# A hybrid encoder: another order of stages, and the recurrence's transposes made by VectorE in 32x32 blocks and moved by DMAs

## The chip, the cores and the metric

The kernel runs on one core of a Trainium2 chip. Its time is the device time of one execution, in microseconds; the median of several executions is given. Profiles show one execution.

## What is computed

The input is 512 tokens of 1024 float32 values. Layer 0 normalises (RMS), projects into a gated MLP branch and a windowed attention branch, and projects the gated branches back. Layer 1 is a gated linear recurrence over 16 heads of 128 channels, in both directions; then a norm per head, a gate, an output projection and a final RMS norm. Cut to layer 1's core:

```
f = lb + (1 - lb) * sigmoid(f_logit);  k = 1 - f;  g = log f
bcum = cumsum of g in a chunk;  q_t = q * exp(bcum);  k_t = k * exp(-bcum)
a = tril(q_t @ k_t.T);  o = a @ v  +  q_t @ state;  state = decay * state + k_end.T @ v
o = o_forward + o_backward;  o = o * rsqrt(mean(o * o) + eps) * gain
x = x + (o * silu(z)) @ w_out;  out = rms_norm(x, final gain)
```

## The kernel before

**Products.** Every large product is float32 split into a high and a low part: high x high, high x low, low x high, three matmuls of 128x512 for each block of 128 rows (`mm3`, L215). Weights come in pieces of 512 KB: a DMA on SP's queue (`_dma`, L53 and L55), a cast to the high part by ScalarE (L66) and the low part by VectorE (L67). Four raw buffers and four split buffers are there; loads are issued seven pieces ahead of use, splits three ahead (`ahead`).

**Two kinds of product.** `t_block` makes one block of 128 channels by 512 tokens from one piece, 24 matmuls. `nat_blocks` makes 512 tokens by 512 channels from four pieces, 96 matmuls. `out_blocks` projects the outputs of some heads back and adds them to the four token tiles `xs` (n heads: 8 blocks of 3n matmuls).

**Layer 1.** Four groups J of four heads. A group first makes the values `iv` and the gates `zv` (two `nat_blocks`, 192 matmuls), then, from the second group on, projects the outputs of earlier heads (`out_blocks`: heads 0 to 3, 4 to 7, and in the last group 8 and 9), then for each head three `t_block`s (query and the two forget gates) and starts the head's recurrence `hgrn`. Behind the last head stand the projections of heads 10 to 13 and of 14 and 15. These last two heads' projection also makes the final norm (`finish`, `store`, L792 to L808).

**The side work.** `hgrn`, layer 0's attention and its mixer are generators: they issue some instructions, then `yield n`, which means "go on after n ticks". A tick comes with every eighth matmul of `mm3` (`SLOT`), and at most three generators run (`tick`, `spawn`, L190 to L205). `tick_until` makes ticks without matmuls until a result is there. So the text fixes where in TensorE's stream each piece of a head stands:

```
prepare q, k (ScalarE, VectorE, POOL)  yield 7   L655-L683
a = masked products; 6 key transposes  yield 1   L692-L710
k.T @ v                                yield 1   L720
state u; a @ v                         yield 1   L731-L735
q @ state                              yield 1   L739-L741
head norm, gate                        yield 4   L746-L751
4 output transposes; split ahi, alo    yield 1   L755-L758
```

The six key transposes (L708, L709) go to PSUM and are copied by ScalarE to `kn` (L710); the four output transposes (L755) go to PSUM, from where ScalarE and VectorE make `ahi` and `alo` (L757, L758). POOL multiplies `qf` into `qb` and `qf` (L680, L682) for heads 0 to 13.

**Order.** The framework plans each engine's order from costs that it estimates: an instruction whose operands are not there yet can be passed by a later one of the same engine. Inside `manual_schedule` the named engines keep the order of the text. On the chip each engine runs its list in that order.

**Layer 0.** `evac_va` (L420) normalises the gated branch's values right behind their products, on VectorE and POOL.

Of the kernel before, what the change touches and what calls it, by code (L numbers as in the profile page):

```python
# [18 lines left out]
P = 128  # L19
S = 512  # L20
# [9 lines left out]
WARM = 10  # L30

# [61 lines left out]
def tile_encoder(ctx, tc, x, xT, nge, wie, lng, lnb, ws, bs, sink, woe, ngo, wio, gaf, gab, hng, woo, fng, out):  # L93
# [89 lines left out]


# [5 lines left out]
    def tick():  # L190
        while waiting and len(side) < 3:
            side.append([waiting.popleft(), 1])
        for job in list(side):
            job[1] -= 1
            if job[1] <= 0:
                try:
                    job[1] = next(job[0])
                except StopIteration:
                    side.remove(job)

    def spawn(gen, delay=1):
        if len(side) < 3:
            side.append([gen, delay])
        else:
            waiting.append(gen)  # L205
# [77 lines left out]
    def act_pair():  # L283
        return [act.tile([P, S], F32R, tag=n, name=n, bufs=6) for n in ("ahi", "alo")]
# [39 lines left out]
    with ExitStack() as c0:  # L324
# [94 lines left out]

        def evac_va(nh):  # L420
            def f(t, ps):
                nc.scalar.copy(va[t][:, ts(nh, 512)], ps)
                nc.vector.bn_stats(out=st[t][:, nh], in_=ps)
                if nh == 1:
                    mv = small.tile([P, 2], F32, tag="mv", name="mv")
                    nc.vector.bn_aggr(out=mv, in_=st[t])
                    v = small.tile([P, 1], F32, tag="lnv", name="lnv")
                    nc.vector.tensor_scalar(out=v, in0=mv[:, 1:2], scalar1=rq2[:, t:t + 1], scalar2=EPS,
                                            op0=ALU.mult, op1=ALU.add)
                    r = inv_sqrt(v, 1, "ln")  # L430
                    nc.gpsimd.tensor_tensor(out=r, in0=r, in1=rq[:, t:t + 1], op=ALU.mult)
                    nc.vector.tensor_scalar(out=va[t], in0=va[t], scalar1=mv[:, 0:1], scalar2=r,
                                            op0=ALU.subtract, op1=ALU.mult)
                    nc.vector.tensor_tensor(out=va[t], in0=va[t], in1=lngb, op=ALU.mult)
                    nc.gpsimd.tensor_tensor(out=va[t], in0=va[t], in1=lnbb, op=ALU.add)
            return f
# [21 lines left out]

        kThi = l0.tile([P, 2, S], F32R, tag="kThi", name="kThi")
# [3 lines left out]
        for j in range(2):  # L463
            ps = t_block()
# [187 lines left out]
    def hgrn(h, sq, sg, iv, zv):  # L652
        hl = h % 4
        hs = ts(hl, P)
# [48 lines left out]
        kn = l1.tile([P, 3, 2, P], F32, tag="kn1", name="kn1", bufs=1)  # L703
        for b in range(2):
            nj = 2 if b == 0 else 1
            ps = sm_bank()
            for j in range(nj):
                nc.tensor.transpose(ps[:, ts(2 * j, P)], ck(kf, 2 * b + j), ident)  # L708
                nc.tensor.transpose(ps[:, ts(2 * j + 1, P)], ck(kb, 3 - 2 * b - j), ident)  # L709
            nc.scalar.copy(kn[:, 2 * b:2 * b + nj].rearrange("p j d t -> p (j d t)"), ps[:, :nj * 256])  # L710
        yield 1
        pk = []
        for b in range(2):
            nj = 2 if b == 0 else 1
            ps = sm_bank()
            for j in range(nj):
                for d in range(2):
                    jj = 2 * b + j
                    n = jj if d == 0 else 3 - jj
                    nc.tensor.matmul(ps[:, ts(2 * j + d, P)], lhsT=kn[:, jj, d], rhs=iv[:, n, hs], start=True, stop=True)  # L720
            pk += [ps[:, j * 256:(j + 1) * 256].rearrange("p (d v) -> p d v", d=2) for j in range(nj)]
        yield 1
# [14 lines left out]
        yield 1  # L737
# [5 lines left out]
        yield 1  # L743
# [19 lines left out]
    for J in range(4):  # L763
        iv = l1.tile([P, NT, 512], F32, tag="iv", name="iv", bufs=2)
        zv = l1.tile([P, NT, 512], F32, tag="zv", name="zv", bufs=2)

        def evac_i(t, ps):
            nc.scalar.copy(iv[:, t], ps)

        def evac_z(t, ps):  # L770
            nc.scalar.activation(zv[:, t], ps, AF.Sigmoid)
            nc.vector.tensor_tensor(out=zv[:, t], in0=ps, in1=zv[:, t], op=ALU.mult)

        nat_blocks(evac_i)
        nat_blocks(evac_z)
        if J:
            n = 2 if J == 3 else 4
            tick_until(lambda: 4 * (J - 1) + n - 1 in acat1)
            out_blocks([acat1[4 * (J - 1) + k] for k in range(n)])
# [12 lines left out]
    def finish(t, nh):  # L792
        if nh == 0:
            sst[t] = small.tile([P, 2], F32, tag="ss", name="ss")
        junk = l1.tile([P, 512], F32, tag="o2", name="junk", bufs=1)
        square_half(t, nh, sst[t], junk)
        if nh == 1:
            if t:
                store(t - 1)
            scales.append(rstd_halves(sst[t], "nr"))  # L800

    scales = []

    def store(t):
        for cs in halves:
            xv = xs[t][:, cs]
            nc.vector.scalar_tensor_tensor(out=xv, in0=xv, scalar=scales[t], in1=gain2[:, cs], op0=ALU.mult, op1=ALU.mult)
            nc.sync.dma_start(out=out[ts(t, P), cs], in_=xv)  # L808

# [38 lines left out]
```

## Time and profile before

| | |
|---|---|
| median of 3 runs | 1029.49 us (1029.46 to 1029.79) |
| the profiled execution | 1029.34 us |
| its span, first to last instruction | 1027.6 us |
| mean granted TensorE clock | 0.997 of full speed |
| layer 1 with the end | from about 372 us on |

The page gives each engine's busy time and instructions; the timeline gives start, duration and operation of each instruction, and in brackets how long its engine stood idle before it and what ended that. Matmuls overlap, so the distance between two starts is read, not the duration of one.

### The profile page before, as it was taken

The page shows a single profiled execution, that of the slowest core. Times are in us where ns is not written, and L with a number is a line of the kernel's source. Part 1 is how long each engine was busy: PE and PEld are TensorE (multiplying, and loading weights), DVE is VectorE, ACT ScalarE, POOL GpSimd, SP SyncE. Part 2 cuts the span into 40 slices and gives each one's busy share as a digit, 9 for nine tenths or more (in the row PEclk, how much of TensorE's full clock was granted, in tenths as well). Part 3 has the DMA queues.
Part 4 walks back from the last instruction along what each step waited for, and adds up shares of the span by engine and source line. Part 5 has one row for each costly group of instructions (what it writes and reads, how often), then busy time and mean ns, then how long its engine had stood idle before and what let it go on. Part 6 is the DMA issues. An engine that isn't in the chain of part 4 may idle for free.

```text
span 1027.6 us, 13580 instructions
## 1 busy us (share of the span) xinstructions
PE 1009.1 (98%) x5363; PEld 847.9 (83%) x5363; DVE 599.9 (58%) x948; ACT 520.2 (51%) x702; POOL 180.3 (18%) x180
## 2 busy tenths in 40 slices
PE   9999999999999999999999999999999999999996
PEld 6888888888888887878888888888888888878884
DVE  5585777575444474347653547754546754547785
ACT  6335656363222154377743258753257753377742
POOL 0320010022133300013321004231003322013101
PEclk9999999999999999999999999999999999999998
DMA  9443121322332313432202441212432223422102
GB/s 347 124 124 103 62 83 42 103 80 65 103 103 83 104 43 104 129 94 75 71 21 82 126 120 42 92 32 82 123 103 62 63 63 103 123 82 83 42 1 82
DMA packets 110527, 91.62 MB, mean 89 GB/s; under 512 B 3280, under 2 KB 88832, under 8 KB 110464
## 3 DMA queue, kind: packets, MB, share of 16 engines
q1 hardware_dynamic: 110224, 90.72, 28.5%
q8 instruction: 42, 0.69, 0.3%
q14 instruction: 21, 0.17, 0.0%
q0 software_dynamic: 96, 0.04, 0.0%
q10 hardware_dynamic: 144, 0.00, 0.0%
HBM read 88.65 MB, written 2.10 MB: 88 GB/s over the span
## 4 chain that ended last, share of the span: by engine, by line
PE 86%; issue 5%; DVE 3%; ACT 3%; POOL 2%; POOLq 0%; DVEq 0%; ACTq 0%
PE mm L215 71%; PE sm L720 2%; PE sm L692 2%; PE sm L495 1%; PE sm L735 1%; PE sm L534 1%; PE sm L741 1%; PE sm L739 1%; DVE c L664 1%; PE sm L523 1%; PE sm L708 1%; PE sm L755 1%; PE sm L561 1%; DVE wlo L67 1%; PE sm L694 1%
## 5 line engine op out<-in xcount | busy, mean ns | idle before, releaser
L66 ACT CAST whi<-wraw 128x1024 fp32r<-128x1024 f32 (+1 forms) x158 | 163.2, 1039 | 224.8 <-PE mm L215 191.7
L67 DVE TENSOR_TENSOR wlo<-wraw,whi 128x1024 fp32r<-128x1024 f32 (+1 forms) x158 | 198.3, 1263 | 124.8 <-ACT whi L66 122.2
L215 PE MATMUL mm<-hhi,wlo 128*128 128x512 f32 x656 | 257.9, 393 | 1.6 <-DVE wlo L67 1.6
L215 PE MATMUL mm<-hlo,whi 128*128 128x512 f32 x656 | 258.1, 393 | 0.0
L215 PE MATMUL mm<-hhi,whi 128*128 128x512 f32 x656 | 256.4, 391 | 0.0
L215 PEld LDWEIGHTS mm<-hhi,wlo 128*128 128x128 f32 x656 | 123.3, 188 | 25.7 <-DVE wlo L67 2.0
L215 PEld LDWEIGHTS mm<-hhi,whi 128*128 128x128 f32 x656 | 123.3, 188 | 24.3
L215 PEld LDWEIGHTS mm<-hlo,whi 128*128 128x128 f32 x656 | 123.3, 188 | 24.1
L215 PE MATMUL mm<-wlo,hhi 128*128 128x512 f32 (+1 forms) x320 | 122.4, 382 | 0.3 <-DVE wlo L67 0.3
L215 PE MATMUL mm<-whi,hlo 128*128 128x512 f32 (+1 forms) x320 | 122.5, 383 | 0.0
L215 PE MATMUL mm<-whi,hhi 128*128 128x512 f32 (+1 forms) x320 | 122.0, 382 | 0.0
L215 PE MATMUL mm<-whi,ahi 128*128 128x512 f32 x256 | 100.4, 392 | 0.1
L215 PE MATMUL mm<-wlo,ahi 128*128 128x512 f32 x256 | 100.2, 392 | 0.0
L215 PE MATMUL mm<-whi,alo 128*128 128x512 f32 x256 | 100.1, 392 | 0.0
L279 DVE TENSOR_TENSOR x<-mm,x 128x512 f32<-128x512 f32 x72 | 49.0, 688 | 44.3 <-PE mm L215 44.2
L680 POOL TENSOR_TENSOR sq<-sq,en 128x512 f32<-128x512 f32 x14 | 23.8, 1702 | 266.4 <-ACT en L672 266.4
L215 PEld LDWEIGHTS mm<-wlo,hhi 128*128 128x128 f32 x320 | 60.3, 188 | 11.9 <-DVE wlo L67 1.1
L215 PEld LDWEIGHTS mm<-whi,hhi 128*128 128x128 f32 x320 | 60.3, 188 | 10.6
L215 PEld LDWEIGHTS mm<-whi,hlo 128*128 128x128 f32 x320 | 60.3, 188 | 10.5
L215 PEld LDWEIGHTS mm<-whi,ahi 128*128 128x128 f32 x256 | 48.1, 188 | 10.1 <-ACT ahi L757 0.5
L215 PEld LDWEIGHTS mm<-whi,alo 128*128 128x128 f32 x256 | 48.1, 188 | 9.6
L215 PEld LDWEIGHTS mm<-wlo,ahi 128*128 128x128 f32 x256 | 48.1, 188 | 9.5
(194 smaller groups left out, 1463.4 us busy)
## 6 DMA issues: line engine op xcount, KB each, us to landing
wraw<-in_w_in_odd_dram SPq DMA_DIRECT2D x80, 512.0 KB, 3.8
wraw<-in_w_in_even_dram SPq DMA_DIRECT2D x42, 512.0 KB, 3.8
wraw<-in_w_out_even_dram SPq DMA_DIRECT2D x16, 512.0 KB, 3.5
wraw<-in_w_out_odd_dram SPq DMA_DIRECT2D x16, 512.0 KB, 3.5
xk<-in_xT_dram SPq DMA_DIRECT2D x8, 256.0 KB, 5.6
x<-in_x_dram SPq DMA_DIRECT2D x4, 512.0 KB, 8.2
out_dram<-x SPq DMA_DIRECT2D x8, 256.0 KB, 2.0
wraw<-in_w_in_even_dram SPq DMA_DIRECT2D x4, 256.0 KB, 4.7
```

The source lines that it names most:

```text
L66: self.nc.scalar.copy(hi[:, j], raw[:, j])
L67: self.nc.vector.tensor_tensor(out=lo[:, j], in0=raw[:, j], in1=hi[:, j].bitcast(F32), op=ALU.subtract)
L215: nc.tensor.matmul(ps, lhsT=l, rhs=r, start=(i == 0), stop=(i == n - 1))
L279: nc.vector.tensor_tensor(out=xv, in0=ps, in1=xv, op=ALU.add)
L495: nc.tensor.matmul(pv, lhsT=a[:, ql], rhs=b[:, kv, kr], start=(i == 0), stop=(i == 2))
L523: nc.tensor.transpose(ps[:, ts(n - n0, P)], pr[:, n, ts(j - KEYS[n][0], P)], ident)
L534: nc.tensor.matmul(po[:, n0 * P:n1 * P], lhsT=a[:, j, ts(kv, P)], rhs=b[:, j, :w], start=(j == 0 and i == 0), stop=(j == NT - 1 and i == 2 ...
L561: nc.tensor.matmul(ps[:, ts(n, P)], lhsT=va[n][:, ts(c, P)], rhs=wsT[:, g], start=True, stop=True)
L664: nc.vector.tensor_tensor_scan(out=cf, data0=reset.rearrange("p n t -> p (n t)"), data1=cf, initial=0.0, op0=ALU.mult, op1=ALU.add)
L680: eng.tensor_tensor(out=v8(qb), in0=v8(qf), in1=en[:, 1, :, 0:64], op=ALU.mult)
L692: nc.tensor.matmul(ps[:H, o:o + P], lhsT=kf[:, lo_:mid], rhs=qf[:, lo_:hi_], start=True, stop=True)
L720: nc.tensor.matmul(ps[:, ts(2 * j + d, P)], lhsT=kn[:, jj, d], rhs=iv[:, n, hs], start=True, stop=True)
```

## The change

Ten of every head's transposes leave TensorE for heads 0 to 12 (`LATE = 13`). Keys: VectorE transposes 32x32 blocks of `kf` and `kb` into `kblk`; `block_move` puts them in place, the four blocks on the diagonal by ScalarE copies of 32 partitions, the twelve others each by a DMA on SP's queue. Outputs likewise, from `o2` by `oblk` to `oT`. `kblk` shares a buffer with `en`. The ticks of these heads are 9, 5, 2, 3, 2, 7; heads 13 to 15 keep 7, 1, 1, 1, 1, 4 and their transposes. `qb` and `qf` are multiplied by VectorE for all heads. Four generators may run, and eight pairs `ahi`, `alo` are held.

The order: heads 8 and 9 are projected behind head 15, not in the last group. Layer 0's normalisation becomes a generator with a wait of two ticks, and the first key block is made before the buffers of that step are taken. The last projection (`last_blocks`) keeps the text's order on VectorE and ScalarE, splits its last block in two halves, and shares the final scaling between VectorE, ScalarE and POOL.

The diff, with unchanged middle parts left out:

```diff
+LATE = 13
...
+    def block_move(dst, blk):
+        for a in range(4):
+            nc.scalar.copy(dst[ts(a, 32), :, ts(a, 32)], blk[ts(a, 32), :, ts(a, 32)])
+            for b in range(4):
+                if a != b:
+                    nc.sync.dma_start(out=dst[ts(b, 32), :, ts(a, 32)], in_=blk[ts(a, 32), :, ts(b, 32)])
...
-        while waiting and len(side) < 3:
+        while waiting and len(side) < 4:
...
-        if len(side) < 3:
+        if len(side) < 4:
...
-        return [act.tile([P, S], F32R, tag=n, name=n, bufs=6) for n in ("ahi", "alo")]
+        return [act.tile([P, S], F32R, tag=n, name=n, bufs=8) for n in ("ahi", "alo")]
...
-        if J:
-            add_out(woo, 4 * (J - 1), 2 if J == 3 else 4)
+        if J in (1, 2):
+            add_out(woo, 4 * (J - 1))
...
+    add_out(woo, 8, 2)
     add_out(woo, 10, 4)
     add_out(woo, 14, 2)
...
+        def layer_norm(t):
+            mv = small.tile([P, 2], F32, tag="mv", name="mv")
+            nc.vector.bn_aggr(out=mv, in_=st[t])
+            v = small.tile([P, 1], F32, tag="lnv", name="lnv")
+            nc.vector.tensor_scalar(out=v, in0=mv[:, 1:2], scalar1=rq2[:, t:t + 1], scalar2=EPS, op0=ALU.mult, op1=ALU.add)
+            r = inv_sqrt(v, 1, "ln")
+            nc.gpsimd.tensor_tensor(out=r, in0=r, in1=rq[:, t:t + 1], op=ALU.mult)
+            yield 2
+            nc.vector.tensor_scalar(out=va[t], in0=va[t], scalar1=mv[:, 0:1], scalar2=r, op0=ALU.subtract, op1=ALU.mult)
+            nc.vector.tensor_tensor(out=va[t], in0=va[t], in1=lngb, op=ALU.mult)
+            nc.gpsimd.tensor_tensor(out=va[t], in0=va[t], in1=lnbb, op=ALU.add)
...
+                    spawn(layer_norm(t))
...
+        ps_k = t_block()
+        tick_until(lambda: not side and not waiting)
         kThi = l0.tile([P, 2, S], F32R, tag="kThi", name="kThi")
...
+        pause = (7, 1, 1, 1, 1, 4) if h >= LATE else (9, 5, 2, 3, 2, 7)
...
-        eng.tensor_tensor(out=v8(qb), in0=v8(qf), in1=en[:, 1, :, 0:64], op=ALU.mult)
+        nc.vector.tensor_tensor(out=v8(qb), in0=v8(qf), in1=en[:, 1, :, 0:64], op=ALU.mult)
         nc.vector.tensor_tensor(out=v8(kb), in0=v8(kb), in1=c[:, 1, :, 0:64], op=ALU.mult)
-        eng.tensor_tensor(out=v8(qf), in0=v8(qf), in1=c[:, 0, :, 1:65], op=ALU.mult)
-        yield 7
+        nc.vector.tensor_tensor(out=v8(qf), in0=v8(qf), in1=c[:, 0, :, 1:65], op=ALU.mult)
+        kn = l1.tile([P, 6, P], F32, tag="kn1", name="kn1", bufs=2)
+        if h < LATE:
+            kblk = l1.tile([P, 6, P], F32, tag="en", name="kblk", bufs=1)
+            for d, src in enumerate((kf[:, :384], kb[:, P:])):
+                nc.vector.transpose(kblk[:, 3 * d:3 * d + 3].rearrange("p n t -> p (n t)"), src)
+            block_move(kn, kblk)
+        yield pause[0]
...
-        kn = l1.tile([P, 3, 2, P], F32, tag="kn1", name="kn1", bufs=1)
-        for b in range(2):
-            nj = 2 if b == 0 else 1
-            ps = sm_bank()
-            for j in range(nj):
-                nc.tensor.transpose(ps[:, ts(2 * j, P)], ck(kf, 2 * b + j), ident)
-                nc.tensor.transpose(ps[:, ts(2 * j + 1, P)], ck(kb, 3 - 2 * b - j), ident)
-            nc.scalar.copy(kn[:, 2 * b:2 * b + nj].rearrange("p j d t -> p (j d t)"), ps[:, :nj * 256])
-        yield 1
+        if h >= LATE:
+            for d in range(2):
+                ps = sm_bank()
+                for j in range(3):
+                    nc.tensor.transpose(ps[:, ts(j, P)], ck((kf, kb)[d], j + d), ident)
+                nc.scalar.copy(kn[:, 3 * d:3 * d + 3].rearrange("p j t -> p (j t)"), ps[:, :384])
+        yield pause[1]
...
-        yield 4
-        ps = sm_bank()
-        for n in range(NT):
-            nc.tensor.transpose(ps[:, ts(n, P)], o2[:, n], ident)
+        if h < LATE:
+            oblk = l1.tile([P, NT, P], F32, tag="oblk", name="oblk", bufs=1)
+            nc.vector.transpose(oblk.rearrange("p n v -> p (n v)"), o2.rearrange("p n v -> p (n v)"))
+            ps = l1.tile([P, NT, P], F32, tag="oT", name="oT", bufs=1)
+            block_move(ps, oblk)
+            ps = ps.rearrange("p n v -> p (n v)")
+            yield pause[5]
+        else:
+            yield pause[5]
+            ps = sm_bank()
+            for n in range(NT):
+                nc.tensor.transpose(ps[:, ts(n, P)], o2[:, n], ident)
...
+        def part(t, i, c0, n):
...
+            mm3(ps[:, :n], ops)
+            xv = xs[t][:, c0:c0 + n]
+            nc.vector.tensor_tensor(out=xv, in0=ps[:, :n], in1=xv, op=ALU.add)
+            nc.scalar.activation(junk[:, :n], xv, AF.Square, scale=1.0 / 32, accum_out=sums[t][:, i:i + 1])
...
+        def store(t):
+            x0 = xs[t][:, :512]
+            nc.vector.scalar_tensor_tensor(out=x0, in0=x0, scalar=scales[t], in1=gain2[:, :512], op0=ALU.mult, op1=ALU.mult)
+            nc.sync.dma_start(out=out[ts(t, P), :512], in_=x0)
+            nc.scalar.activation(xg[t], xg[t], AF.Copy, scale=scales[t])
+            nc.sync.dma_start(out=out[ts(t, P), 512:], in_=xg[t])
+
+        for t in range(NT):
+            sums[t] = small.tile([P, 4], F32, tag="ss", name="ss")
+            part(t, 0, 0, 512)
+            if t:
+                scales[t - 1] = inv_sqrt(first_sums(t - 1), 1, "nr")
+            part(t, 1, 512, 512 if t < NT - 1 else 256)
+            if t < NT - 1:
+                nc.gpsimd.tensor_tensor(out=xg[t], in0=xs[t][:, 512:], in1=gain2[:, 512:], op=ALU.mult)
             if t:
                 store(t - 1)
...
+        part(t, 2, 768, 256)
...
+        r = inv_sqrt(v, 1, "nr")
+        nc.vector.tensor_tensor(out=xg[t][:, :512], in0=x1, in1=gain2[:, 512:], op=ALU.mult)
+        nc.scalar.activation(x0, x0, AF.Copy, scale=r)
+        nc.vector.tensor_scalar(out=xg[t][:, :512], in0=xg[t][:, :512], scalar1=r, scalar2=None, op0=ALU.mult)
...
+    tick_until(lambda: 9 in acat1)
+    out_blocks([acat1[8], acat1[9]])
     tick_until(lambda: 13 in acat1)
     out_blocks([acat1[k] for k in range(10, 14)])
     tick_until(lambda: 15 in acat1)
-    with tc.manual_schedule(engines={mybir.EngineType.DVE}):
-        out_blocks([acat1[14], acat1[15]], finish)
-        store(NT - 1)
+    with tc.manual_schedule(engines={mybir.EngineType.DVE, mybir.EngineType.Activation}):
+        last_blocks([acat1[14], acat1[15]])
```

## Rows read from the trace of the kernel before

**Rows 1.** The page, part 1: busy time, share and instructions of each engine.

```profile
PE 1009.1 (98%) x5363; PEld 847.9 (83%) x5363; DVE 599.9 (58%) x948; ACT 520.2 (51%) x702; POOL 180.3 (18%) x180
```

**Rows 2.** Waits of TensorE: who waited for whom, total us, times, longest.

```profile
PE sm L692 <- POOL sq L682: 4.1, 4, 1.0
```

**Rows 3.** Timeline in layer 0, VectorE and TensorE: start us, us, instruction [idle before].

```profile
51.53 0.82 DVE L432 TENSOR_SCALAR va<-va,mv,lnr 128x1024 f32<-128x1024 f32 x1 [2.25 <-POOL lnr L431]
...
51.57 0.39 PE L215 MATMUL mm<-hlo,whi 128*128 128x512 f32 x1
53.53 0.50 PE L215 MATMUL mm<-hhi,wlo 128*128 128x512 f32 x1 [1.57 <-DVE wlo L67]
```

**Rows 4.** Timeline of TensorE at the end of the recurrence and at its last product.

```profile
1007.55 0.39 PE L215 MATMUL mm<-whi,alo 128*128 128x512 f32 x1
1008.85 0.63 PE L755 MATMUL sm<-ident,o 128*128 128x128 f32 x4 [0.91 <-DVE o L751]
...
1009.78 0.40 PE L215 MATMUL mm<-whi,alo 128*128 128x512 f32 x1
1010.25 0.51 PE L215 MATMUL mm<-whi,ahi 128*128 128x512 f32 x1
...
1018.33 0.39 PE L215 MATMUL mm<-whi,alo 128*128 128x512 f32 x1
```

**Rows 5.** Timeline of TensorE, first key transpose of a head and the next large product.

```profile
948.55 0.33 PE L708 MATMUL sm<-ident,sg 128*128 128x128 f32 x1
...
949.18 0.47 PE L215 MATMUL mm<-hlo,whi 128*128 128x512 f32 x1
```

**Rows 6.** Timeline of TensorE, the output transposes of a head.

```profile
866.44 0.60 PE L755 MATMUL sm<-ident,o 128*128 128x128 f32 x4
866.79 0.47 PE L215 MATMUL mm<-whi,hlo 128*128 128x512 f32 x1
867.11 0.39 PE L215 MATMUL mm<-whi,hhi 128*128 128x512 f32 x1
```

**Rows 7.** Timeline of TensorE ahead of L692 in the last group.

```profile
922.89 0.39 PE L215 MATMUL mm<-hhi,whi 128*128 128x512 f32 x1
924.28 0.32 PE L692 MATMUL sm<-sq,sg 128*64 128x128 f32 x1 [1.00 <-POOL sq L682]
```

**Rows 8.** Groups by line and shape: count | busy us, mean ns | idle before.

```profile
L682 DVE TENSOR_TENSOR sq<-sq,c 128x512 f32<-128x512 f32 x2 | 1.4, 688 | 0.0
L710 ACT COPY kn<-sm 128x512 f32<-128x512 f32 x16 | 9.3, 582 | 24.6 <-PE sm L709 24.6
L710 ACT COPY kn<-sm 128x256 f32<-128x256 f32 x16 | 6.0, 376 | 0.0
```

**Rows 9.** Busy us by engine: second head of a group; the projections between groups.

```profile
core 0: us, PE busy (x) PEld busy (x) DVE busy (x) ACT busy (x) POOL busy (x), PEclk, DMA share, GB/s
484.30:507.00 22.70, 22.70 (x148) 19.37 (x147) 16.43 (x28) 16.91 (x21) 7.03 (x7) 1.00 0.23 71
552.50:596.00 43.50, 43.50 (x194) 35.99 (x193) 18.86 (x22) 12.03 (x14) 0.00 (x0) 1.00 0.34 97
```

**Rows 10.** Timeline of SP's queue at the start: issues of loads.

```profile
1.24 0.90 SPq L53 DMA_DIRECT2D wraw<-in_w_in_even_dram  x2
2.18 0.91 SPq L344 DMA_DIRECT2D xk<-in_xT_dram  x2
...
15.03 0.34 SPq L363 DMA_DIRECT2D lnbb<-in_gmlp_ln_b_dram  x1
16.31 0.33 SPq L363 DMA_DIRECT2D bsb<-in_gmlp_b_s_dram  x1
```

**Rows 11.** The page, part 6: issues of the output's stores, KB each, us to landing.

```profile
out_dram<-x SPq DMA_DIRECT2D x8, 256.0 KB, 2.0
```

**Rows 12.** Timeline of the last head's norm, after its last product.

```profile
1004.11 0.60 ACT L746 ACTIVATE o<-sm 128x512 f32<-128x512 f32 x1 [8.47 <-PE sm L741]
...
1006.82 0.69 DVE L750 TENSOR_TENSOR o<-sm,hrr 128x512 f32<-128x512 f32 x1 [1.19 <-POOL hrr L150]
```

**Rows 13.** Timeline of VectorE in the tail.

```profile
1019.44 1.29 DVE L279 TENSOR_TENSOR x<-mm,x 128x512 f32<-128x512 f32 x2
...
1022.83 1.42 DVE L807 SCALAR_TENSOR_TENSOR x<-x,nrr,gain 128x512 f32<-128x512 f32 x2 [0.66 <-POOL nrr L150]
```

More of the change, by code (lines that the diff above doesn't have):

```diff
@@ L424, in f @@
                 if nh == 1:
[L425 to L435, printed above, removed]
+                    spawn(layer_norm(t))
             return f
@@ L463, in tile_encoder @@
         for j in range(2):
-            ps = t_block()
+            ps = t_block() if j else ps_k
             kt = l0.tile([P, S], F32, tag="zt", name="kt", bufs=2)
@@ L719, in hgrn @@
                     n = jj if d == 0 else 3 - jj
-                    nc.tensor.matmul(ps[:, ts(2 * j + d, P)], lhsT=kn[:, jj, d], rhs=iv[:, n, hs], start=True, stop=True)
+                    nc.tensor.matmul(ps[:, ts(2 * j + d, P)], lhsT=kn[:, jj if d == 0 else 5 - jj], rhs=iv[:, n, hs], start=True, stop=True)
             pk += [ps[:, j * 256:(j + 1) * 256].rearrange("p (d v) -> p d v", d=2) for j in range(nj)]
-        yield 1
+        yield pause[2]
         u = l1.tile([P, 3, 2, P], F32, tag="u", name="u", bufs=1)
@@ L736, in hgrn @@
                              skip_group_check=True)
-        yield 1
+        yield pause[3]
         for j in range(3):
@@ L742, in hgrn @@
                              skip_group_check=True)
-        yield 1
+        yield pause[4]
         o2 = l1.tile([P, NT, P], F32, tag="o2", name="o2", bufs=1)
@@ L775, in tile_encoder @@
         nat_blocks(evac_z)
[L776 to L779, printed above, removed]
+        if J in (1, 2):
+            tick_until(lambda: 4 * J - 1 in acat1)
+            out_blocks([acat1[4 * (J - 1) + k] for k in range(4)])
         for h in range(4 * J, 4 * J + 4):
@@ L791, in tile_encoder, with last_blocks, first_sums @@
     nc.sync.dma_start(out=gain2, in_=fng.partition_broadcast(P))
-    def finish(t, nh):
-        if nh == 0:
-            sst[t] = small.tile([P, 2], F32, tag="ss", name="ss")
+    def last_blocks(heads):
+        pieces = [W.take() for _ in range(2)]
         junk = l1.tile([P, 512], F32, tag="o2", name="junk", bufs=1)
-        square_half(t, nh, sst[t], junk)
-        if nh == 1:
+        xg = [l1.tile([P, 512], F32, tag=tag, name="xg", bufs=1 if tag != "kn1" else 2) for tag in ("u", "kn1", "asum", "en")]
+        sums, scales = {}, {}
+        def part(t, i, c0, n):
+            ps = mm_bank()
+            ops = []
+            nh, cs = c0 // 512, slice(c0 % 512, c0 % 512 + n)
+            for k, (ahi, alo) in enumerate(heads):
+                whi, wlo = pieces[nh]
+                a, b = ahi[:, ts(t, P)], alo[:, ts(t, P)]
+                ops += [(a, whi[:, k, cs]), (a, wlo[:, k, cs]), (b, whi[:, k, cs])]
+            mm3(ps[:, :n], ops)
+            xv = xs[t][:, c0:c0 + n]
+            nc.vector.tensor_tensor(out=xv, in0=ps[:, :n], in1=xv, op=ALU.add)
+            nc.scalar.activation(junk[:, :n], xv, AF.Square, scale=1.0 / 32, accum_out=sums[t][:, i:i + 1])
+        def first_sums(t):
+            v = small.tile([P, 1], F32, tag="nrv", name="nrv")
+            ss = sums[t]
+            nc.vector.tensor_scalar(out=v, in0=ss[:, 0:1], scalar1=ss[:, 1:2], scalar2=EPS, op0=ALU.add, op1=ALU.add)
+            return v
+        def store(t):
[12 more added lines that the diff above has]
+                nc.gpsimd.tensor_tensor(out=xg[t], in0=xs[t][:, 512:], in1=gain2[:, 512:], op=ALU.mult)
@@ L798, in finish @@
             if t:
                 store(t - 1)
[L800 to L808, printed above, removed]
+        t = NT - 1
+        part(t, 2, 768, 256)
+        v = first_sums(t)
+        x0, x1 = xs[t][:, :512], xs[t][:, 512:]
@@ new lines, in last_blocks @@
+        nc.vector.tensor_tensor(out=x0, in0=x0, in1=gain2[:, :512], op=ALU.mult)
+        nc.vector.tensor_scalar(out=v, in0=sums[t][:, 2:3], scalar1=v, scalar2=None, op0=ALU.add)
+        r = inv_sqrt(v, 1, "nr")
+        nc.vector.tensor_tensor(out=xg[t][:, :512], in0=x1, in1=gain2[:, 512:], op=ALU.mult)
+        nc.scalar.activation(x0, x0, AF.Copy, scale=r)
+        nc.vector.tensor_scalar(out=xg[t][:, :512], in0=xg[t][:, :512], scalar1=r, scalar2=None, op0=ALU.mult)
+        nc.sync.dma_start(out=out[ts(t, P), 512:], in_=xg[t][:, :512])
@@ L810, in tile_encoder @@
+        nc.sync.dma_start(out=out[ts(t, P), :512], in_=x0)
+    tick_until(lambda: 9 in acat1)
+    out_blocks([acat1[8], acat1[9]])
     tick_until(lambda: 13 in acat1)
```

## The prediction

> **What bounds the kernel now.** I read the engine totals first: TensorE is busy 98% of the span, the next engine 58% [rows 1]. So the time is TensorE's instruction stream plus the places where that stream stands still, and a change is worth what it takes out of the stream, what it takes out of the stops, and what it takes off the ends. The 128x512 products follow each other every 0.23 us, which is the unit in all the gaps below.
>
> Then I went through TensorE's timeline for starts that are further apart than the work between them. There are few: four stops ahead of the first attention-like products of a head (L692), each put down to POOL's multiply L682 by the list of waits [rows 2], one in layer 0 [rows 3], two beside the last head's output transposes [rows 4]. Past them comes the tail: the last product starts at 1018.33, the span ends at 1027.6 [rows 4].
>
> The sum below is made against the profiled execution, 1029.34 us (span 1027.6 and 1.7 around it); the median of the three runs is 1029.49, so the two can be used as one.
>
> **The change part by part.**
>
> (a) *Transposes leave TensorE for heads 0 to 12.* The six key transposes take from 948.55 to the next product at 949.18, 0.63 us [rows 5]. The four output transposes take from 866.44 to 866.79, and the product after them is spaced 0.32 instead of 0.23, so 0.44 us [rows 6]. The switch after the keys stays, since the small products ahead of them stay. 13 x (0.63 + 0.44) = 13.9 us, all of it in the stream that sets the end.
>
> (b) *The stop at L692.* The product at 922.89 should have been followed 0.23 us later, and L692 starts at 924.28: 1.16 us lost [rows 7], at the first head of each of the four groups, 4.6 us. The change waits 9 ticks instead of 7 there (a tick is eight products, 1.8 us, so 3.6 us more cover), and heads 0, 4, 8 and 12 all fall under it. It also moves both multiplies of `qf` and `qb` to VectorE, where one takes 0.69 us [rows 8] in place of 1.5 to 1.7 on POOL. The whole 4.6 us should go. What is late next there: nothing of PE's, but VectorE gets the work (see d).
>
> (c) *Layer norm of layer 0.* At 51.57 the stream stops until 53.53, less 0.23: 1.7 us, behind a `wlo` that stands in VectorE's queue after a normalisation waiting for POOL [rows 3]. With the normalisation two ticks later, the splits are ahead of it. I take 1.7 us; bounds 0 (another small operation takes its place) and 1.7. The additional wait until no side job is left falls after a full key block of 24 products, 5.4 us, which covers it.
>
> (d) *What replaces the transposes.* Per head VectorE gets two multiplies and three block transposes (384, 384 and 512 wide). The trace shows no such transpose; the nearest row is a 512-wide VectorE operation at 0.69 us [rows 8], so I take 0.69 for each, bounds half and double. 5 x 0.69 = 3.5 us on top of 16.4 in a busy head of 22.7 [rows 9]: 19.9 of the 21.6 us that a head lasts without its transposes (22.7 less 1.07). ScalarE loses two copies (0.58 and 0.38) and gets eight of 32 partitions, at most 0.58 each: 16.9 + 4.6 - 1.0 = 20.5 at the worst. Neither is over, and the later heads and the two long projections of each group, where VectorE has 18.9 of 43.5 us [rows 9], give room. Cost on the path: nothing, covered by splits that run ahead of their use; if that cover is gone each microsecond of overrun is paid. Bounds 0 and 1 us a head.
>
> (e) *24 moves a head on SP's queue*, behind and ahead of the weight loads. Consecutive issues at the start are 0.47 us apart, the least; small loads that wait for something are 1.28 apart [rows 10]. At 0.47 the moves take 11.3 us of a head's 21.6, with the weight loads 12.7. The queue waits at each first move for VectorE's transpose, and a weight load behind it is held up; a load held up by 11 us still has four weight pieces of cover. A store lands 2.0 us after issue [rows 11], so keys are back about 8 us after their transpose; they have 14 ticks. Outputs have 7 ticks, 13 us. Cost: nothing, bounds below.
>
> (f) *The two output projections after the first and second group.* The last head of the group now needs some 29 ticks, and the two long projections ahead give 24. From its last product to its gated output's scale it takes 3.4 us (ACT start 1004.11 to the end of L750 at 1007.51) [rows 12], then 1.5 for the POOL multiply, 0.7 for the transpose, 12 x 0.47 + 2.0 for the moves, 0.7 for the split: 14 us. The last product of that head stands 32 products, 7.3 us, ahead of the projection, and the projection can do three heads of a block, 2.0 us, before it needs the fourth; if the compiler's order lets all four banks start, 8.2 us. So the stop is between 0 and 4.7 us, twice. The order is planned and the planner missed 1.16 us in (b), so I take 1 us each: 2 us lost. A stop behind these on ScalarE holds casts of weights; 1 us more for all such.
>
> (g) *End of the recurrence.* Heads 8 and 9's projection (48 products, 10.9 us) moves behind head 15, which then has 144 products instead of 96 ahead of it. The two stops of 1.07 and 0.24 us [rows 4] go: 1.3 us.
>
> (h) *Tail.* Now VectorE adds, scales and multiplies alone: its last add begins at 1019.44, the last scale only at 1022.83 and runs 1.42 us [rows 13]. The change gives half of the scaling to ScalarE and POOL, halves the last block and scales its two halves side by side. Add 0.42, square 0.6, sum 0.2, power 0.6, scale 0.65, issue 0.35 and 2.0 to land, then the same 1.3 to the end (estimates from the same operations at half width): 6.4 us after the last product, where 1018.7 to 1027.6 is 8.9. Gain 2.5, bounds 1 and 3.5. Six more instructions of half width: 0 to 1.4 us on TensorE, taken as 0.
>
> Sum: 13.9 + 4.6 + 1.7 + 1.3 + 2.5 = 24.0 gained, 3 lost: 21 us. 1029.3 - 21 = 1008.3, forecast **1008 us**.
>
> One rule speaks against (a). The row shows ten transposes of TensorE at 0.11 us apiece beside VectorE and ScalarE each about three quarters full. By the Trainium skill, "VectorE: DVE Perf Modes", section Rules for kernel authors, a 128x128 transpose belongs on TensorE if a PSUM destination is acceptable, and VectorE is for 32x32 blocks only. By row, 1.07 us a head of the full engine is worth more than 3.5 us of one that has room; by the rule, the change would lose. That case is the third rival.
>
> **The rivals.**
>
> *Late outputs.* The moves land later than planned, and (f) is paid in full, 4.7 us twice, with 3 us of stopped casts besides: 1008 + 2 x 3.7 + 2 = 1017. For it: the 29 ticks against 24. Against: four banks can start, and the outputs' own chain is short. Chance 0.25.
>
> *The order edits do nothing.* The stops of (b), (c) and (g) come back at another instruction, because the side chain is now longer and VectorE fuller; only (a) and (h) are left: 1029.3 - 16.4 + 3 = 1016. Against: each stop has its own cover, worked out above. Chance 0.08, inside the range of the first.
>
> *SP's queue becomes the pace: slower.* Moves and weight loads share one in-order queue. If a move takes 1.3 us, like the spacing of 1.28 at the start [rows 10], a head needs 24 x 1.3 + 1.1 = 32.3 us of SP, 10.7 over; after four heads 43 us late, of which the ticks cover about 13, so some 30 us of stop in each of three groups: 1005 + 90 = 1095. It decides from about 1.0 us a move (four heads x (24 x 1.0 + 1.1 - 21.6) = 14 us late, 7 of them covered, three times, with the rest of the gain eaten by (f)). For it: 24 moves in place of ten instructions. Against: the 0.47 of the back-to-back issues. Chance 0.10. Beside it: by the Trainium skill, "DMA: Bandwidth & Descriptors", section Rules for kernel authors, transfers under 64 KB are mostly overhead; a move here carries 16 to 24 KB, and no row shows one.
>
> **How the numbers follow.** Forecast as it stands 0.57, late outputs 0.25, order edits lost 0.08, slower 0.10. A measurement of this kernel tells 0.2%, 2 us, from no change. The first three are all faster, but 0.03 of them may be eaten down to no change: faster 0.87, same 0.03, slower 0.10. The range: downward, all of (f) free, the tail at 3.5 and nothing lost: 1029.3 - 25 = 1004, and a little for transposes that cost more than their spacing (the switch of 0.09 at each group): 1002. Upward it takes in the late outputs and lost edits with a little more: 1021. That leaves out the slower cases and a little on both sides.
>
> **What would show it.** L708, L709 and L755 on TensorE for heads 13 to 15 only (30 instructions instead of 160); a head's period 21.6 instead of 22.7 us; no wait of L692; VectorE near 90% in the second head of a group; SP's moves at 0.47 us; tail 6.4 us after the last product. Wrong would be a stop of over 5 us ahead of the output projections, SP's moves at over 0.9 us, or TensorE waiting for `wlo` or `kn` in the heads.

## The result, and the profile after

The changed kernel takes 1072.4 us (median; 1071.1 to 1074.6) where the kernel before, on the same chip, takes 1029.6: ratio 1.0418, 95% interval 1.0405 to 1.0431. It is 4.2% slower, where 1008 us was forecast with a range to 1021. The forecast was wrong in sign. The profiled execution spans 1069.5 us.

The engine totals of the changed kernel (busy us, share, instructions), against [rows 1], and its transfers of blocks (page, part 6: KB each, us to landing):

```profile
PE 1013.9 (95%) x5239; PEld 845.3 (79%) x5239; DVE 629.2 (59%) x1015; ACT 548.2 (51%) x790; POOL 147.7 (14%) x155
...
kn<-kblk SPq DMA_DIRECT2D x156, 24.0 KB, 1.9
oT<-oblk SPq DMA_DIRECT2D x156, 16.0 KB, 1.8
```

VectorE and ScalarE are no fuller than the forecast had them (in a busy head, 484.3 to 505.0 us, 17.0 and 16.4 of 20.7 us, where 19.9 and at worst 20.5 of 21.6 were forecast). TensorE has 124 instructions fewer and still fell from 98% to 95%. So it stands still more. Its waits in the changed kernel (who waited for whom, total us, times, longest), against [rows 2]:

```profile
PE mm L224 <- ACT whi L67: 26.8, 3, 9.7
PE mm L224 <- ACT ahi L785: 6.7, 2, 3.5
...
PE mm L224 <- DVE x L288: 3.0, 1, 3.0
```

The wait of L692 for POOL is gone, as forecast. In its place stand three long waits for a cast of weights (`whi`), one in the first projections of each later group, and two for an output (`ahi`) at the out projections. What ScalarE did ahead of the first of them, in its timeline, and below it VectorE's transpose of head 1's output:

```profile
528.97 1.22 ACT L188 COPY oT<-oblk 32x128 f32<-32x128 f32 x4
...
535.15 1.04 ACT L67 CAST whi<-wraw 128x1024 fp32r<-128x1024 f32 x1
546.99 0.72 ACT L785 ACTIVATE ahi<-oT,gm 128x512 fp32r<-128x512 f32 x1 [10.79 <-DMA oT<-oblk]
547.61 0.57 ACT L796 COPY iv<-mm 128x512 f32<-128x512 f32 x1
548.08 1.04 ACT L67 CAST whi<-wraw 128x1024 fp32r<-128x1024 f32 x1
```

```profile
527.42 0.66 DVE L774 STREAM_TRANSPOSE oblk<-o 128x512 f32<-128x512 f32 x1
```

ScalarE stands for 10.79 us at the split of head 1's moved output. The evacuation of a block and the cast that TensorE needs next are behind it in ScalarE's queue. SP's queue over the same stretch, and TensorE:

```profile
527.55 8.02 SPq L191 DMA_DIRECT2D kn<-kblk  x12
535.68 7.02 SPq L191 DMA_DIRECT2D oT<-oblk  x11
...
543.38 0.59 SPq L191 DMA_DIRECT2D oT<-oblk  x1
```

```profile
540.08 0.39 PE L224 MATMUL mm<-whi,hlo 128*128 128x512 f32 x1
549.18 0.80 PE L224 MATMUL mm<-whi,hhi 128*128 128x512 f32 x1 [8.71 <-ACT whi L67]
...
551.03 0.63 PE L224 MATMUL mm<-whi,hlo 128*128 128x512 f32 x1
551.46 0.63 PE L224 MATMUL mm<-whi,hhi 128*128 128x512 f32 x1
```

Head 1's twelve output moves are issued only after head 3's twelve key moves, one every 0.64 us (7.02 / 11), and the last lands 18.6 us after VectorE's transpose. After the stop the products come 0.43 us apart (551.03 to 551.46) instead of 0.23. The stretches behind the stop (columns: PE, PEld, DVE, ACT and POOL busy, granted clock, DMA share, GB/s):

```profile
540.00:549.20 9.20, 0.49 (x4) 0.07 (x2) 1.40 (x3) 2.14 (x3) 0.00 (x0) 0.67 0.54 169
549.20:551.20 2.00, 1.53 (x3) 0.93 (x4) 1.18 (x1) 0.00 (x0) 1.96 (x1) 0.50 0.17 66
551.20:553.20 2.00, 2.00 (x8) 1.61 (x7) 0.71 (x1) 0.82 (x3) 0.32 (x1) 0.50 0.68 256
553.20:555.20 2.00, 2.00 (x15) 1.87 (x15) 1.05 (x3) 1.96 (x4) 0.00 (x0) 0.97 0.18 31
```

The granted clock fell to the lower of its two levels (0.50 of 2.4 GHz) while TensorE stood, and stayed there for some 4 us of products after it. So this stop cost more than its length. Counted from start to start, as in the prediction, and leaving out the first 10 us, stops of over 0.4 us sum to 49 us (before: 8) and the smaller gaps, mostly such slow products, to 15 (before: 2). The stream without them is some 11 to 13 us shorter than in the run of the order alone, below, by how the smaller gaps are counted.

The tail, against [rows 13] and the last line of [rows 4]: the last product and the last store's issue.

```profile
1061.31 0.28 PE L224 MATMUL mm<-whi,alo 128*128 128x256 f32 x1
...
1062.57 0.42 DVE L838 TENSOR_TENSOR x<-mm,x 128x256 f32<-128x256 f32 x1
...
1066.04 0.38 SPq L874 DMA_DIRECT2D out_dram<-xg  x1
```

### The profile page after: what moved, and what is told of

It is laid out like the page before. It is cut to its first block, busy times and chain, and to the rows that moved or that the text cites. A ratio compares the mean times of both kernels' runs of the same rounds, so it can differ in the third digit from the quotient of the medians.

```text
span 1069.5 us, 13935 instructions
## 1 busy us (share of the span) xinstructions
PE 1013.9 (95%) x5239; PEld 845.3 (79%) x5239; DVE 629.2 (59%) x1015; ACT 548.2 (51%) x790; POOL 147.7 (14%) x155
## 5 line engine op out<-in xcount | busy, mean ns | idle before, releaser
L224 PE MATMUL mm<-wlo,hhi 128*128 128x512 f32 (+1 forms) x320 | 124.7, 390 | 1.7 <-DVE wlo L68 1.7
L224 PE MATMUL mm<-whi,ahi 128*128 128x512 f32 (+1 forms) x258 | 103.7, 402 | 9.7 <-ACT ahi L785 6.7
L224 PE MATMUL mm<-wlo,ahi 128*128 128x512 f32 (+1 forms) x258 | 103.3, 401 | 0.3 <-DVE wlo L68 0.2
L224 PE MATMUL mm<-whi,alo 128*128 128x512 f32 (+1 forms) x258 | 102.8, 400 | 0.0
L288 DVE TENSOR_TENSOR x<-mm,x 128x512 f32<-128x512 f32 x64 | 43.6, 687 | 41.6 <-PE mm L224 41.6
L785 ACT ACTIVATE ahi<-oT,gm 128x512 fp32r<-128x512 f32 x13 | 9.4, 723 | 83.6 <-DMA oT<-oblk 83.6
```

The source lines that it names most:

```text
L224: nc.tensor.matmul(ps, lhsT=l, rhs=r, start=(i == 0), stop=(i == n - 1))
L288: nc.vector.tensor_tensor(out=xv, in0=ps, in1=xv, op=ALU.add)
L785: nc.scalar.activation(ahi, ps, AF.Copy, scale=hg[:, h:h + 1])
```

## The experiments

Line numbers in the diffs' kernels differ by one or two from the changed kernel's. All ratios are to the kernel before.

**1. The order alone.**

```diff
-LATE = 13
+LATE = 0
```

> All sixteen heads are transposed by TensorE again, with the short pauses; the new order of stages, VectorE's share of the small products and the new tail stay. Theory (the loss comes from the moves alone): no stop behind the recurrence's key buffer (4 x 1.16 us gone, as in the changed kernel) and a tail 0.9 us shorter, so about 1024 us, between 1019 and 1030. Rival A (the new order is at fault: the stage order leaves the projections without cast weights): the stops of 8 to 10 us at the starts of groups stay, 1050 us or more.

Measured: 1026.6 us, ratio 0.9974 (0.9964 to 0.9984). Rival A falls: the loss comes with the moves. The order edits are worth 2.9 us. TensorE's waits for the masked block products and for the out projection:

```profile
PE mm L224 <- DVE x L288: 1.8, 1, 1.8
...
PE sm L714 <- DVE sq L698: 1.1, 4, 0.3
```

**2 and 3. Keys alone, outputs alone.**

```diff
-        if h < LATE:      # output's block transpose (run 2); key's (run 3)
+        if h < 0:
```

> Only the keys are moved (12 moves a head); the outputs of all heads are transposed by TensorE, pauses as in the changed kernel. Theory (ScalarE stands in order at the copy of the moved output, with the weight casts behind it): no moved output, so no stop over 3 us at 540, 710 and 881 us, and beside the order alone the 13 x 0.63 us of key transposes gone: 1012 to 1024 us. Rival B (12 moves a head by one queue, and VectorE's and ScalarE's extra work, are themselves too much): at least a third of the loss of 43 us is left, 1045 us or more.

> Only the outputs are moved (12 moves a head); the keys are transposed by TensorE, pauses as in the changed kernel. Theory (outputs are late because SP issues a move every 0.645 us and the outputs' 12 stand behind another head's 12): with the queue free an output needs 12 x 0.645 + 1.9 = 9.6 us in place of up to 17, so ScalarE's stops at that copy shrink from 10 to 11 us to 2 to 4 us and the stops of TensorE at the group starts with them: 1022 to 1040 us. Rival C (it is ScalarE's order alone, however long the queue: the copy is placed before the casts and waits for any move): stops of 6 us or more stay, 1050 us or more.

Measured: keys alone 1026.7 us, ratio 0.9976 (0.9966 to 0.9987); outputs alone 1056.9, ratio 1.0263 (1.0248 to 1.0278). Against the order alone the moved keys cost 0.2 us, the moved outputs 30.3, both 45.8; so the loss hangs on the outputs, and another 15 us on both together. Run 2 missed its forecast: the stream without its gaps got some 8 us shorter, as expected (8.2), but new stops ate that. TensorE's timeline in run 2 where heads 12 and 13 meet (two of five stops):

```profile
925.10 0.55 PE L729 MATMUL sm<-ident,sg 128*128 128x128 f32 x3 [1.38 <-DVE u L748]
...
950.67 0.66 PE L783 MATMUL sm<-ident,o 128*128 128x128 f32 x4 [1.48 <-POOL o L771]
```

Run 3 speaks against a long queue as the whole cause, and for rival C. SP takes an output's moves at once, and ScalarE (its timeline) has the split only one evacuation behind the block copies:

```profile
525.96 1.22 ACT L188 COPY oT<-oblk 32x128 f32<-32x128 f32 x4 [2.84 <-DVE oblk L774]
527.20 0.58 ACT L796 COPY iv<-mm 128x512 f32<-128x512 f32 x1
535.39 0.72 ACT L785 ACTIVATE ahi<-oT,gm 128x512 fp32r<-128x512 f32 x1 [7.60 <-DMA oT<-oblk]
```

For ScalarE not to wait, moves and landing would have had to take 1.8 us from the first block copy (525.96 to 527.78); the split starts 9.4 us after it. Over the 13 heads of run 3 the outputs land 8.9 to 13.9 us after their transpose, no later than (e) allowed but for one, and ScalarE still waits 61.6 us for them.

**4 and 6. The split on another engine.** First the first half on GpSimd, then both halves.

```diff
-        nc.scalar.activation(ahi, ps, AF.Copy, scale=hg[:, h:h + 1])
+        nc.gpsimd.tensor_scalar(out=ahi, in0=ps, scalar1=hg[:, h:h + 1], scalar2=None, op0=ALU.mult)
```

> As the changed kernel, but the scaled copy of a moved output (first half of the split) is taken by GpSimd in place of ScalarE for heads 0 to 12: nothing on ScalarE waits for an output's moves any more. Theory (the casts held behind that copy make the stops of 8.5 to 9.8 us at the starts of groups 1 to 3, and the low clock after them): those three stops go, with the slow products behind them; the stops before the out projections (3.4 and 3.65 us), which need the late outputs themselves, stay or grow by 1 us: 1028 to 1042 us. Rival B (the queue of moves itself, or the fullness of VectorE): the stops stay in another dress, 1060 us or more.

> As the changed kernel, but both halves of the split of a moved output are taken by GpSimd for heads 0 to 12 (three instructions: scale, round, subtract). In the run with only the first half on GpSimd the second half stood on VectorE and held the low parts of the weights behind it (23.6 us of TensorE's waits by VectorE's wlo). Theory (any engine that feeds TensorE loses if it stands in order at a moved output): now neither ScalarE nor VectorE stands, the waits of TensorE for whi, wlo and kn go: 1030 to 1048 us. Rival D (the stop moves with the copy to GpSimd, which holds the masked sums and the gate of the next head behind it): TensorE waits for asum or o for as long, 1055 us or more.

Measured: 1072.7 us (1.0424; 1.0404 to 1.0444) and 1091.3 (1.0597; 1.0581 to 1.0613). Both expectations of the theory missed. In run 4 VectorE's timeline shows why: it stands at the second half, which needs the first.

```profile
535.77 1.22 DVE L68 TENSOR_TENSOR wlo<-wraw,whi 128x1024 fp32r<-128x1024 f32 x1
545.93 0.75 DVE L789 SCALAR_TENSOR_TENSOR alo<-oT,gm,ahi 128x512 fp32r<-128x512 f32 x1 [8.94 <-DMA wraw<-in_w_out_odd_dram]
...
547.39 1.22 DVE L68 TENSOR_TENSOR wlo<-wraw,whi 128x1024 fp32r<-128x1024 f32 x1
```

(The releaser named there is not the one; `ahi` on GpSimd, from 544.32 to 545.89, came last.) In run 6 neither ScalarE nor VectorE waits for a move itself, and rival D holds by a detour. GpSimd's and VectorE's timelines:

```profile
550.00 1.57 POOL L786 TENSOR_SCALAR oT<-oT,gm 128x512 f32<-128x512 f32 x1 [10.12 <-DMA oT<-oblk]
551.55 1.03 POOL L151 TENSOR_TENSOR hrr<-hrv,mhalf 128x4 f32<-128x4 f32 x1
```

```profile
552.61 0.69 DVE L770 TENSOR_TENSOR o<-sm,hrr 128x512 f32<-128x512 f32 x1 [11.64 <-POOL hrr L151]
553.22 1.22 DVE L68 TENSOR_TENSOR wlo<-wraw,whi 128x1024 fp32r<-128x1024 f32 x1
```

GpSimd stands at the moved output, with the next head's small power behind it; VectorE waits for that power, and the low part of the weights stands behind VectorE's wait. TensorE waits 37.6 us for `wlo` in all. Taking the split off ScalarE does not free the weights.

**5. The split written down later.**

```diff
-            yield pause[5]
+            yield pause[5] if h == 12 else 12
```

> As the changed kernel, but the split of a moved output is written down five ticks later for heads 0 to 11 (12 in place of 7; a tick is 8 products, so about 40 x 0.22 = 8.7 us later in the order in which ScalarE gets its work); all moves stay as they are. Theory (the loss is ScalarE's order: the copy stands ahead of the weight casts while the moves are still on their way): the casts of a group's first weights now stand ahead of the copy, the stops at 540, 710 and 881 us (8.9, 9.8 and 8.5 us) go to under 3 us each and the slow products behind them go too: 1028 to 1048 us. The stops at the out projections (3.4 and 3.65 us) stay. Rival B (the queue of 24 moves a head is too long by itself, or VectorE too full): 1060 us or more.

Measured: 1071.4 us, ratio 1.0413 (1.0398 to 1.0429). The run decides nothing between the two: in the trace all 630 copies, casts and activations of ScalarE come in the same order as in the changed kernel. So the written place did not set that order: the plan put the split where it had been.

**7. Through DRAM.**

```diff
-        for a in range(4):
-            nc.scalar.copy(...)        # 4 copies, 12 moves
+        d = dp.tile([4, 32, n, 4, 32], F32, tag=f"d{n}", name=f"d{n}", bufs=2)
+        nc.sync.dma_start(out=d.rearrange("a p n b t -> (a p) n (b t)"), in_=blk)
+        for b in range(4):
+            nc.sync.dma_start(out=dst[ts(b, 32)].rearrange("p n (a t) -> p n a t", a=4),
+                              in_=d[:, :, :, b].rearrange("a p n t -> p n a t"))
```

> As the changed kernel, but the blocks travel through DRAM: one transfer of the whole tile out and four back (one for each 32 partitions of the target), in place of 12 moves and four ScalarE copies: 10 transfers a head on SP in place of 24, and no 8 small copies on ScalarE. Theory (the number of moves at 0.645 us each makes the outputs late): SP's share falls from 15.5 to 10 x 0.645 = 6.5 us a head; a tile is there after one issue, a transfer, four issues and a transfer, about 0.6 + 2 + 4 x 0.645 + 2 = 7 us in place of 9.6 and of up to 17 behind another head's: stops over 5 us go, 1020 to 1040 us. Rival C (ScalarE's order alone: any transfer, of 7 us too, is waited for with the casts behind): 1045 us or more.

Measured: 1028.2 us, ratio 0.9990 (0.9981 to 0.9999), 44 us under the changed kernel and inside the forecast, but not for the reason expected, so the hit is luck. SP's queue and ScalarE's timeline for head 1, and the list of ScalarE's waits:

```profile
523.09 0.34 SPq L190 DMA_DIRECT2D d<-oblk  x1
...
537.84 1.92 SPq L192 DMA_DIRECT2D oT<-d  x3
```

```profile
536.92 1.05 ACT L67 CAST whi<-wraw 128x1024 fp32r<-128x1024 f32 x1
...
541.89 0.60 ACT L798 ACTIVATE zv<-mm 128x512 f32<-128x512 f32 x1 [2.61 <-PE mm L223]
543.01 0.72 ACT L784 ACTIVATE ahi<-oT,gm 128x512 fp32r<-128x512 f32 x1 [0.53 <-DMA oT<-d]
```

```profile
ACT ahi L784 <- DMA oT<-d: 4.5, 5, 1.5
```

The output comes back as late as before: the split starts 19.9 us after VectorE's transpose, at whose end the first transfer is issued (523.09 to 543.01), and 18.9 us after the transpose in the changed kernel. Over the 13 heads the outputs land 13.2 us after their transpose on the mean, in the changed kernel 13.7. Only here the casts and two more instructions stand ahead of it in ScalarE's order, and ScalarE waits 4.5 us for all outputs in place of 83.6.

**8. A sharper border.**

```diff
-        pause = ... else (9, 5, 2, 3, 2, 7)     # on run 2
+        pause = ... else (9, 4, 1, 1, 1, 4)
```

> Keys moved, outputs transposed by TensorE, and the long pauses shortened to (9, 4, 1, 1, 1, 4), so that head 13, which has short ones, no longer runs into head 12's steps. In the run with the keys moved alone five stops of 1.5, 0.9, 1.0, 1.3 and 1.6 us lay where heads 12 and 13 overlap (923 to 950 us). Theory (these 6.3 us ate the 13 x 0.63 = 8.2 us that the key transposes give back): 1018 to 1022 us. Rival E (the stream does not get shorter when key transposes leave it): 1025 us or more.

Measured: 1044.8 us, ratio 1.0151 (1.0134 to 1.0167): a miss. The time is over rival E's bound, but not for its reason: without its gaps the stream is as short as in run 2. The short pauses put the products of nearly every head ahead of their own `u`:

```profile
PE sm L759 <- DVE u L751: 12.7, 11, 2.1
```

So pauses this short do not do where keys are moved; lengths in between were not tried for all heads.

**9. The same moves, the split anchored behind the casts.**

```diff
-        nc.scalar.activation(ahi, ps, AF.Copy, scale=hg[:, h:h + 1])
+        sc = small.tile([P, 1], F32, tag="hgc", name="hgc", bufs=2)
+        nc.gpsimd.tensor_scalar(out=sc, in0=anchor[0], scalar1=0.0, scalar2=hg[:, h:h + 1], op0=ALU.mult, op1=ALU.add)
+        nc.scalar.activation(ahi, ps, AF.Copy, scale=sc)
```

`anchor[0]` is a column of the block evacuated last, at a place 12 ticks behind the moves.

> As the changed kernel, all 24 moves a head on SP's queue kept, but the scale of the split of a moved output now depends on the projection block evacuated last before a place 12 ticks behind the moves (one GpSimd instruction of 128x1: 0 x that block's column + the gain), so that ScalarE cannot get the copy ahead of that block, whatever its planned order makes of the moves; ScalarE's order in the program then has the casts of a group's first weights ahead of it. Theory (the loss is the copy's place in ScalarE's order, not the time that the moves take): the stops at the group starts (8.9, 9.8 and 8.5 us) go, with the slow products behind them (some 15 us); the stops at the out projections (3.4 to 3.7 us) stay: 1030 to 1045 us. Rival B (24 moves a head on SP are too many, wherever the copy stands): 1060 us or more.

Measured: 1041.6 us, ratio 1.0115 (1.0099 to 1.0132): 31 us less, with every move in place. ScalarE's and TensorE's lines:

```profile
536.45 1.06 ACT L67 CAST whi<-wraw 128x1024 fp32r<-128x1024 f32 x1
...
541.82 0.60 ACT L805 ACTIVATE zv<-mm 128x512 f32<-128x512 f32 x1 [3.01 <-PE mm L224]
545.57 0.73 ACT L790 ACTIVATE ahi<-oT,hgc 128x512 fp32r<-128x512 f32 x1 [3.16 <-POOL hgc L789]
```

```profile
PE mm L224 <- ACT ahi L790: 14.5, 4, 6.0
```

No wait for `whi` is left beside one of 0.5 us at the start. What is left are mainly the out projections, 14.5 us, more than the 6.7 before, since the split was put off. Heads 2 and 6 had landed 8 us before their split; and as the one buffer `oT` is held until then, the moves of heads 3 and 7 begin 6.8 us after their transpose, where it was 0.1 in the changed kernel.

**10 and 11. Repairs of the run through DRAM.** Softened pauses; then also the out projections of groups 0 and 1 one head later (loads of weights moved with them).

```diff
+        pause = {13: (8, 4, 1, 3, 1, 4), 14: (8, 2, 1, 2, 1, 4), 15: (7, 1, 1, 1, 1, 4)}.get(h, (9, 5, 2, 3, 2, 7))
...
-        if J in (1, 2):
-            tick_until(lambda: 4 * J - 1 in acat1)
-            out_blocks([acat1[4 * (J - 1) + k] for k in range(4)])
         for h in range(4 * J, 4 * J + 4):
+            if h in (5, 9):
+                tick_until(lambda: 4 * J - 1 in acat1)
+                out_blocks([acat1[4 * (J - 1) + k] for k in range(4)])
```

> The transfers through DRAM, and the pauses of heads 13 and 14 shortened step by step, (8, 4, 1, 3, 1, 4) and (8, 2, 1, 2, 1, 4), so that head 13 does not run into head 12. With the transfers through DRAM alone TensorE still stopped 1.3, 1.0, 1.3 and 1.7 us where heads 12 and 13 overlap and 2.7 to 2.9 us three times before products of an out projection. Theory: the first four go, 1023 us (1021 to 1026). Rival E (they only move, as with the shortened pauses of the run before): 1027 us or more.

> As the run with the softened pauses, and the out projections of groups 0 and 1 come one head's projections later (after head 4 and head 8 in place of before them), so that their last head's output has 9 ticks more. Theory: the two stops of 2.9 and 2.7 us and the slow products behind them go too: 1017 us (1014 to 1021), which beats the kernel before and the changed one. Rival: the next head's steps collide with the out projection's adds on VectorE, 1023 us or more.

Measured: 1019.9 us (0.9905; 0.9890 to 0.9919), then 1010.0 (0.9810; 0.9796 to 0.9825). Both better than expected; the second beats the kernel before by 1.9%. Its engine totals, and of TensorE's waits the longest and the only one left in the recurrence:

```profile
PE 995.0 (99%) x5239; PEld 835.3 (83%) x5239; DVE 631.0 (63%) x1015; ACT 517.2 (51%) x686; POOL 148.7 (15%) x155
```

```profile
PE mm L223 <- DVE wlo L68: 1.9, 2, 1.6
...
PE sm L758 <- DVE u L750: 0.8, 1, 0.8
```

**12. The moves with all three repairs**: run 9 with the edits of 10 and 11.

> All 24 moves a head kept on SP's queue, with the three repairs together: ScalarE's copy of a moved output placed behind the casts (the anchor), the pauses of heads 13 and 14 softened, the out projections of groups 0 and 1 one head later. Theory (what the moves themselves cost, once nothing that feeds TensorE stands behind them, is next to nothing): the stops left in the anchored run (15 us at the out projections, 6 us at heads 12 and 13) go with the slow products behind them: 1010 to 1017 us, within 0.7% of the run through DRAM with the same two repairs (1010.0 us). Rival B (15.5 us a head of issues on SP, the 8 small ScalarE copies and the later weights still cost): 1022 us or more.

Measured: 1014.4 us, ratio 0.9851 (0.9835 to 0.9868). Rival B falls: 24 moves a head at 0.64 us, the small ScalarE copies and the held-up weights cost at most the 4.3 us by which this is over run 11, once no cast stands behind a moved output that is still on its way.

## Why the prediction was wrong

The step that failed is **(e)**, "Outputs have 7 ticks, 13 us. Cost: nothing", and with it the last sentence of **(f)**, which took 1 us for all casts held on ScalarE. Two things were wrong there.

The price of a move: 0.47 us by [rows 10], measured 0.64, so 15.5 us of SP a head in place of 11.3. Six of the 13 outputs stand behind another head's keys and land 15.1 to 19.0 us after their transpose, not within 13; the other seven land within 8.9 to 13.4. This alone was not what cost: in run 7 outputs come as late and in run 12 the moves are the same, and neither loses by them. The rival on SP's queue had the right sign for the wrong reason; it decided only from 1.0 us a move. The rival of late outputs named stopped casts, but at 3 us, where 27 were measured (the three stops below).

The place of the wait: the 7 ticks were read as 13 us between the moves and the split. They order what is written down, not ScalarE's queue. In the changed kernel ScalarE came to the split 3.2 to 10.7 us after the transpose (head 1: 8.1, from 528.08 to 546.99 less the 10.79 idle), in run 3 one evacuation behind the block copies, and a later written place changed nothing (run 5). So ScalarE waited 83.6 us in all, and where the next cast of weights stood behind it, TensorE stopped: 8.9, 9.8 and 8.5 us. None of the prediction's signs of being wrong named this wait: SP's moves stayed under 0.9 us, and the stops at the out projections under 5. Run 9 changes this place and no move, and 31 of the 46 us go. That shows the cause of these 31; the other 15 went in run 12 with the two further repairs. Why the planned order takes the moves to be that short was not looked into.

The rest by steps. **(a)** held: without its stops run 11's stream is 13.9 us shorter than that of the order alone (995.3 against 1009.2, the last product's end less all gaps; other counts of the small gaps give up to 14.4), against 13.9 forecast. **(b)** held, with the 9 ticks: no wait of that line in runs 10 to 12; with 7 ticks (run 1) 0.44 us each is left. **(c)** failed: VectorE's planned order did not change, and the stop of [rows 3] stands at 1.58 us beside 1.57, behind a split that still follows VectorE's wait for POOL, as the timeline of the changed kernel has it:

```profile
52.05 0.81 DVE L438 TENSOR_SCALAR va<-va,mv,lnr 128x1024 f32<-128x1024 f32 x1 [2.26 <-POOL lnr L436]
...
54.05 0.50 PE L224 MATMUL mm<-hhi,wlo 128*128 128x512 f32 x1 [1.58 <-DVE wlo L68]
```

The same mistake as in (e): a written delay was taken for a place in an engine's queue. **(d)** held; a transpose of 384 takes 0.55 us and of 512 0.71 (estimate 0.69), and in run 11's recurrence TensorE waits for VectorE once, 0.8 us. The transposes in the changed kernel:

```profile
L703 DVE STREAM_TRANSPOSE kblk<-sg x26: 524/548/573, 462.4 to 945.7; 128x384 f32<-128x384 f32 x26
L774 DVE STREAM_TRANSPOSE oblk<-o x13: 658/711/715, 504.5 to 1001.6; 128x512 f32<-128x512 f32 x13
```

(columns: least, median and most ns, first and last start). **(f)** was under-sized at the out projections too: 3.4 and 3.7 us in place of 1 each, inside its bounds of 0 and 4.7. **(g)** failed: its two stops went, but a new one behind VectorE's addition came, of 2.0 us in run 1 and 3.2 in the changed kernel; in run 11 it is gone. **(h)** was over-sized: 0.9 us in place of 2.5. From the last product's end (1061.59) to 1069.55 it is 8.0 us, where 8.9 was before and 6.4 was forecast; the forecast's own terms add up to 6.1, not 6.4. The last addition starts 1.0 us after the last product's end, since VectorE has the scale of the block before it in its queue.

So the gains were there once the wait was gone: in run 11, 13.9 of (a), 4.6 of (b), 1.3 of (g) and some 1 of (h), less a new stop of 1.0, make 19.8 us; measured were 19.5.

By the Trainium skill, "DMA: Bandwidth & Descriptors", section Rules for kernel authors, small transfers are best gathered into large ones. The way out agrees: a key tile in one transfer of 384 KB lands in 2.3 us, one block of 24 KB in 1.9. The whole trip does not show it: with the way back in four pieces the outputs of run 7 landed about as late as those of twelve small moves.

```profile
d<-kblk SPq DMA_DIRECT2D x13, 384.0 KB, 2.3
```

By the Trainium skill, "VectorE: DVE Perf Modes", section Rules for kernel authors, this transpose belongs on TensorE. Run 11 differs: with the transposes off a TensorE that is 99% busy, and the stops repaired, it is 16.5 us faster than the run of the order alone. 13.9 of these are the shorter stream; the others are small stops that the order alone still has, and its repair with TensorE's transposes kept was not tried.

## What to carry to other kernels

When work is moved from the fullest engine to a transfer, price the wait at whatever reads the transfer, on the in-order queue where it stands, and look at what is queued behind it: an engine that is half idle still stops the full one if it stands in front of its feed. Look in the trace for where the reader really comes in that queue; a pause in the written order is no such place, and a true dependence (the anchor) is. Once that is right, the time the transfer takes matters only where its result is used at once: here the out projections had to move one head later. A long stop can cost more than its length: behind the three of 8.5 to 9.8 us some 4 us of products ran at the lower clock, and behind that of 3.4 us at 585 us more than 5 us, but behind one of 2.65 us in run 7 (at 978 us) none.

## What was not expected of the hardware

SP issues a block move every 0.64 us, while [rows 10] has loads of whole tiles 0.47 apart. A trip out to DRAM and back, five transfers, brought an output back about as late as twelve direct moves with four copies (13.2 and 13.7 us on the mean, queueing included). After a stop of 8.7 us the granted clock was 0.50 for about 4 us of products, 0.43 us apart.
